# The last block of a down projection, with its norm, scaling and stores, done for 128 tokens and then for the other 128

## The chip, the cores and the metric

The kernel runs on one core of one Trainium2 chip. The metric is the device time of one execution, in microseconds (us); given are the median and the ends of three runs. The engines are PE (TensorE's products; PEld is its loading of weights), DVE (VectorE), ACT (ScalarE), POOL (GpSimd) and SP (SyncE, whose queue issues most DMAs).

## The reference, cut to what matters

One layer of a diffusion backbone with D_MODEL = 2048 channels and 256 tokens. The end of it is a SwiGLU FFN with 5632 hidden units, a gated residual and a last RMSNorm over the channels of each token:

```python
def rmsnorm(x, w):
    xf = x.astype(jnp.float32)
    y = xf * lax.rsqrt(jnp.mean(xf * xf, axis=-1, keepdims=True) + NORM_EPS)
    return (y * w.astype(jnp.float32)).astype(x.dtype)

def swiglu(h, w_gate_up, w_down):
    gate, up = jnp.split(h @ w_gate_up, 2, axis=-1)
    return (jax.nn.silu(gate) * up) @ w_down
...
        x = x + gt2 * swiglu(modulate(rmsnorm(x, norm2_w[layer]), sh2, sc2),
                             ffn_w_gate_up[layer], ffn_w_down[layer])
...
    return rmsnorm(x, final_norm_w)
```

The change touches the product with `w_down`, the residual and the last `rmsnorm`, no other part.

## The kernel before

Activations lie with channels on the 128 partitions and tokens along the free dimension (T = 256). A product takes 128 x 128 weights as its stationary operand and moves 256 token columns past them. All big products are done in a type that PE multiplies in one pass, fp32r, with two parts for each operand: a rounded high part and the rest. Three products stand for one exact one (`gemm`, L436 to L438): high weights by high activations, high weights by low activations, low weights by high activations. In the trace an fp32r product is one record, and each has its own load of weights (LDWEIGHTS, on PEld).

The weights come from HBM as fp32. `load_w` loads pieces of at most 8 chunks of 128 x 128 into a raw buffer (`wraw`, three of them, SP queue, L421); ACT casts the piece to the high part (`whi`, L426), and DVE subtracts for the low part (`wlo`, L427). There are two buffers of `whi` and two of `wlo`, so ACT's cast of a piece waits until PE is done with the piece two before it, and a load waits until DVE is done with the raw piece three before it.

The down projection (L1981 to L1991) is a loop over 16 blocks j of 128 output channels. Each sums 44 chunks of the hidden units (`Z`: `za` holds the first 32, `zb` the other 12), 132 products into one PSUM bank `mm`; its pieces have 7, 7, 8, 7, 7 and 8 chunks. Then DVE adds the gated result to the residual x1 (L1987), ACT squares it (L464), DVE adds the square to `ssum` (L1990, not for the last block), and ACT multiplies the block by its norm weights (L1991). After the loop `rms_scale` sums the squares over the partitions with two fp32 products by a matrix of ones into the bank `pa` (L455; the first takes `ssum`, the second the last block's square) and takes r by Ln and Exp on ACT (L457, L458). Five scalings on DVE multiply x1 by r (L1994), 4, 4, 4, 2 and 2 blocks of channels each, and each is followed by its store (L1995, SP queue).

`x1`, `ssum`, the squares and r are slices of one buffer, which the trace calls `arena`; `CR` holds the ones, `mod` the gates, `PR` the norm weights. `Hf` (`hfh`, `hfl`) is the input of the FFN, 16 x 256 columns for each of its two parts, last read by the products of the up projection.

The order of the instructions of each engine is set by a scheduler at build time, from its own estimate of a timeline; at run time each engine goes through its own in that order.

Of the kernel before, what the change touches and what calls it, by code (L numbers as in the profile page):

```python
# [328 lines left out]
def emit(ctx: ExitStack, tc, A, out, dbg=None):  # L329
# [29 lines left out]
    def p_(name, i=None, rows=P):  # L359
        lo, hi = _P[name]  # L360
        if i is None:
            return PR[:rows, lo:hi]
        return PR[:rows, lo + i:lo + i + 1]
# [14 lines left out]
    def pst(pool, tag, shape=None):  # L378
        return pool.tile([P, 512], F32, tag=tag, name=tag)
# [27 lines left out]
    def load_w(src, M, nk, kchunk=8, ks=0, into=None):  # L407

        res = []
        pieces = -(-(nk - ks) // kchunk)  # L410
        ends = [ks + (nk - ks) * (i + 1) // pieces for i in range(pieces)]
        for k0, k1 in zip([ks] + ends, ends):
            n = k1 - k0
            if into is None:
                raw = wpool[0].tile([P, 8, P], F32, tag="wraw", name="wraw", bufs=wbufs[0])
                hi = wpool[0].tile([P, 8, P], F32R, tag="whi", name="whi", bufs=wbufs[1])
                lo = wpool[0].tile([P, 8, P], F32R, tag="wlo", name="wlo", bufs=wbufs[2])
            else:
                raw = into[2].tile([P, 8, P], F32, tag="wr", name="wr")
                hi, lo = (t[:, k0:k1] for t in into[:2])  # L420
            ld = Q.dma_start(raw[:, :n, :M], src[:, k0:k0 + n, :])  # L421
            if into is not None:
                tc.keep_in_program_order(ld)
            for i in range(0, n, wstep[0]):
                c = slice(i, min(i + wstep[0], n))
                S.copy(hi[:, c, :M], raw[:, c, :M])  # L426
                V.tensor_sub(lo[:, c, :M], raw[:, c, :M], hi[:, c, :M].bitcast(F32))  # L427
            for k in range(n):
                res.append((k0 + k, hi[:, k, :M], lo[:, k, :M]))
        return res  # L430

    def gemm(ps, wt, X, n, first=True, last=True):

        Xh, Xl = X
        for i, (k, hi, lo) in enumerate(wt):
            E.matmul(ps, hi, Xh[:, k, :n], start=first and i == 0, stop=False)  # L436
            E.matmul(ps, hi, Xl[:, k, :n], start=False, stop=False)  # L437
            E.matmul(ps, lo, Xh[:, k, :n], start=False, stop=last and i == len(wt) - 1)  # L438

    def split(hi, lo, src):  # L440
        S.copy(hi, src)
        V.tensor_sub(lo, src, hi.bitcast(F32))
# [1491 lines left out]
    with tc.tile_pool(name="fp", bufs=1, reuse_waits="tile") as fp:  # L1934
        Hf = (fp.tile([P, KT, T], F32R, name="hfh"), fp.tile([P, KT, T], F32R, name="hfl"))
        s2 = x1p.tile([P, 16], F32, name="s2")
        V.scalar_tensor_tensor(s2, mod[:, 64:80], 1.0, p_("n2"), ALU.add, ALU.mult)
        for k in range(KT):
            hb = x1p.tile([P, T], F32, tag="m", name="hb")
            V.scalar_tensor_tensor(hb, x1[:, k, :], s2[:, k:k + 1], r, ALU.mult, ALU.mult)  # L1940
            S.activation(Hf[0][:, k, :], hb, AF.Identity, bias=mod[:, 48 + k:49 + k])
            V.scalar_tensor_tensor(Hf[1][:, k, :], hb, mod[:, 48 + k:49 + k], Hf[0][:, k, :].bitcast(F32),
                                   ALU.add, ALU.subtract)
        p4 = [pst(pmm, "mm") for _ in range(2)]
        for k in range(KT):
            for a in range(4):

                gemm(p4[a // 2][:, T * (a % 2):T * (a % 2) + T], w4[a][k:k + 1], Hf, T,
                     k == 0 and a % 2 == 0, k == KT - 1 and a % 2 == 1)
        Z = (zap.tile([P, 2, 32, T], F32R, tag="za", name="za"), fp.tile([P, 2, NH - 32, T], F32R, name="zb"))  # L1950
        cb = x1p.tile([P, 4, 512], F32, name="cb")
        Q.dma_start(cb, A["cvec"].partition_broadcast(P).rearrange("p (a d) -> p a d", a=4))
        graw = x1p.tile([P, 16, 4], F32, name="graw")
        for j in range(NH):
            if j < 2:
                ps = p4[j]
            else:
                ps = pst(pmm, "mm")
                gemm(ps[:, 0:T], load_w(A["wgu"][2 * j], P, KT), Hf, T)
                gemm(ps[:, T:512], load_w(A["wgu"][2 * j + 1], P, KT), Hf, T)  # L1960
            g = fp.tile([P, T], F32, tag="g", name="g", bufs=2)
            S.activation(g, ps[:, 0:T], AF.Silu)
            V.tensor_mul(g, ps[:, T:512], g)
            split(Z[j // 32][:, 0, j % 32], Z[j // 32][:, 1, j % 32], g)
            if j == 1:
                tc.keep_in_program_order(S.activation(cb, cb, AF.Silu))
            if 2 <= j < 34:

                for a in range(2):
                    c = (j - 2) // 2  # L1970
                    i = 2 * (j % 2) + a
                    w = fp.tile([P, 512], F32, tag="aw", name="aw", bufs=3)
                    S.dma_start(w, A["ada_gt2"][c, :, 512 * i:512 * i + 512])
                    tc.keep_in_program_order(V.scalar_tensor_tensor(w, w, 1.0, cb[:, i, :], ALU.mult, ALU.mult,
                                                                    accum_out=graw[:, c, i:i + 1]))

        V.tensor_add(graw[:, :, :2], graw[:, :, :2], graw[:, :, 2:])
        V.tensor_add(graw[:, :, 0], graw[:, :, 0], graw[:, :, 1])
        V.tensor_add(mod[:, 80:96], graw[:, :, 0], p_("bada")[:, 80:96])
        tc.keep_in_program_order(S.preload_act_table_set(LNEXP))  # L1980
        for j in range(KT):  # L1981
            ps = pst(pmm, "mm")
            wt = load_w(A["wdn"][j], P, NH)
            for i, z in enumerate(Z):
                gemm(ps[:, 0:T], [(k - 32 * i, hi, lo) for k, hi, lo in wt if k // 32 == i],
                     (z[:, 0], z[:, 1]), T, i == 0, i == 1)
            V.scalar_tensor_tensor(x1[:, j, :], ps[:, 0:T], mod[:, 80 + j:81 + j], x1[:, j, :], ALU.mult, ALU.add)  # L1987
            sq = square_sum(x1p, x1[:, j, :], ssum, j == 0)
            if 0 < j < KT - 1:
                V.tensor_add(ssum, ssum, sq)  # L1990
            S.activation(x1[:, j, :], x1[:, j, :], AF.Identity, scale=p_("nf", j))  # L1991
        r = rms_scale(x1p, [ssum, sq], T, "rs")
        for k0, k1 in ((0, 4), (4, 8), (8, 12), (12, 14), (14, 16)):
            V.tensor_mul(x1[:, k0:k1], x1[:, k0:k1], r.unsqueeze(1).to_broadcast([P, k1 - k0, T]))  # L1994
            Q.dma_start(out[:, k0:k1, :], x1[:, k0:k1, :])  # L1995


def layouts(x, c, ctx, c_ctx, w_ada, b_ada, norm1_w, w_in, rw_mu, rw_w0, rw_w2, rw_a0, rw_a2,
# [93 lines left out]
```

## Time and profile before

| what | value |
|---|---|
| median of 3 runs | 2189.06 us (2189.04 to 2196.04) |
| the profiled execution, first to last instruction (span) | 2188.6 us; the page gives no other time for it, so the runs' median stands 0.4 us above its span |
| PE busy | 2108.6 us, 96% of the span, 24536 products |
| DVE, ACT busy | 1552.5 us, 1118.2 us |
| mean granted clock of PE | 0.986 of full speed |
| from the last product of the down projection to the end | 2176.97 to 2188.63, 11.66 us |

Busy time is the time in which an engine has an instruction running; the ends of matmuls are modelled, so their pace is read from their starts. The stretch in the last line is the only one of some length at the end in which PE has almost nothing to do.

### The profile page before, as it was taken

How to read it: one execution, taken by the hardware profiler on the slowest of the kernel's cores; microseconds unless marked ns; L12 is line 12 of the kernel's file. 1: busy time of each engine (PE TensorE's matmuls, PEld its weight loads, DVE VectorE, ACT ScalarE, POOL GpSimd, SP SyncE). 2: the span in 40 equal slices, each digit the busy share in tenths (PEclk: the TensorE clock that was granted, in tenths of full speed). 3: DMA queues.
4: the chain of work that ended last, by engine and by line, in shares of the span. 5: the costliest groups of instructions: out<-in, count | busy, mean ns of one | idle time of the engine just before them, and what ended most of it. 6: DMA issues, size and time to landing. Idle time of an engine off the chain costs nothing.

```text
span 2188.6 us, 59116 instructions
## 1 busy us (share of the span) xinstructions
PE 2108.6 (96%) x24536; PEld 1977.7 (90%) x24536; DVE 1552.5 (71%) x3308; ACT 1118.2 (51%) x2209; POOL 19.2 (1%) x55
## 2 busy tenths in 40 slices
PE   7999999999999999999999998999999999999997
PEld 5897698889888888998989987999999999999997
DVE  4466589889889976899998776865666665555554
ACT  3246654565455556565565754644444444444443
POOL 0000000000000000000000000000000000000000
PEclk9999999999999999999999999999999999999999
DMA  9966756645555554665653754856777776666665
GB/s 377 415 175 196 228 154 179 178 144 156 154 167 143 166 164 135 188 194 171 176 152 112 216 153 157 297 177 201 238 248 235 242 241 217 194 191 194 195 194 163
DMA packets 276286, 431.14 MB, mean 197 GB/s; under 512 B 119857, under 2 KB 136625, under 8 KB 271665
## 3 DMA queue, kind: packets, MB, share of 16 engines
q1 hardware_dynamic: 262192, 402.19, 59.5%
q10 hardware_dynamic: 13824, 25.17, 3.6%
q8 instruction: 192, 3.15, 0.6%
q14 instruction: 78, 0.63, 0.1%
HBM read 401.50 MB, written 25.77 MB: 195 GB/s over the span
## 4 chain that ended last, share of the span: by engine, by line
PE 80%; DVE 7%; DMA 7%; ACT 3%; issue 2%; SPq 0%; DVEq 0%; ACTq 0%
PE mm L164 26%; PE mm L438 12%; PE mm L436 12%; PE mm L437 12%; PE s L164 6%; PE pa L164 5%; PE pi L164 3%; DVE arena L164 2%; DMA wraw<-w 2%; DVE wlo L164 2%; DMA wraw<-ada_rest 1%; PE mm L529 1%; PE s L579 1%; ACT arena L164 1%; PE mm L579 1%
## 5 line engine op out<-in xcount | busy, mean ns | idle before, releaser
L427 DVE TENSOR_TENSOR wlo<-wraw,whi 128x1024 fp32r<-128x1024 f32 (+1 forms) x264 | 314.9, 1193 | 291.0 <-ACT whi L426 291.0
L426 ACT CAST whi<-wraw 128x1024 fp32r<-128x1024 f32 (+1 forms) x264 | 270.6, 1025 | 386.1 <-PE mm L437 359.5
L164 PE MATMUL mm<-hxh,wlo 128*128 128x256 f32 x1376 | 399.9, 291 | 9.5 <-DVE wlo L164 7.7
L164 PE MATMUL mm<-hxh,whi 128*128 128x256 f32 x1376 | 397.0, 288 | 2.3 <-ACT whi L164 1.3
L164 PE MATMUL mm<-hxl,whi 128*128 128x256 f32 x1376 | 395.4, 287 | 0.0
L438 PE MATMUL mm<-hfh,wlo 128*128 128x256 f32 x1344 | 371.8, 277 | 0.2 <-DVE wlo L427 0.2
L436 PE MATMUL mm<-hfh,whi 128*128 128x256 f32 x1344 | 371.2, 276 | 0.0
L437 PE MATMUL mm<-hfl,whi 128*128 128x256 f32 x1344 | 371.2, 276 | 0.0
L164 ACT CAST whi<-wraw 128x512 fp32r<-128x512 f32 (+1 forms) x398 | 242.8, 616 | 214.9 <-PE mm L164 93.2
L164 DVE TENSOR_TENSOR wlo<-wraw,whi 128x512 fp32r<-128x512 f32 (+1 forms) x398 | 270.3, 682 | 86.2 <-ACT whi L164 79.8
L164 PEld LDWEIGHTS mm<-hxh,wlo 128*128 128x128 f32 x1376 | 260.7, 189 | 19.6 <-DVE wlo L164 11.3
L164 PEld LDWEIGHTS mm<-hxh,whi 128*128 128x128 f32 x1376 | 260.6, 189 | 10.3 <-issue 4.3
L164 PEld LDWEIGHTS mm<-hxl,whi 128*128 128x128 f32 x1376 | 260.8, 190 | 6.3 <-issue 3.9
L438 PEld LDWEIGHTS mm<-hfh,wlo 128*128 128x128 f32 x1344 | 252.4, 188 | 1.2 <-DVE wlo L427 0.8
L437 PEld LDWEIGHTS mm<-hfl,whi 128*128 128x128 f32 x1344 | 252.5, 188 | 0.0
L436 PEld LDWEIGHTS mm<-hfh,whi 128*128 128x128 f32 x1344 | 252.4, 188 | 0.0
L164 PE MATMUL mm<-hch,wlo 128*128 128x256 f32 x496 | 142.5, 287 | 0.0
L164 PE MATMUL mm<-hcl,whi 128*128 128x256 f32 x496 | 142.2, 287 | 0.0
L436 PE MATMUL mm<-za,whi 128*128 128x256 f32 x512 | 141.5, 276 | 0.0
L164 PE MATMUL mm<-hch,whi 128*128 128x256 f32 x496 | 141.3, 285 | 0.2 <-issue 0.2
L438 PE MATMUL mm<-za,wlo 128*128 128x256 f32 x512 | 141.3, 276 | 0.0
L437 PE MATMUL mm<-za,whi 128*128 128x256 f32 x512 | 141.3, 276 | 0.0
(407 smaller groups left out, 4534.2 us busy)
## 6 DMA issues: line engine op xcount, KB each, us to landing
wraw<-w SPq DMA_DIRECT2D x344, 256.0 KB, 3.3
wraw<-wgu SPq DMA_DIRECT2D x168, 512.0 KB, 4.7
aw<-ada_first SPq DMA_DIRECT2D x32, 1024.0 KB, 12.2
wraw<-wdn SPq DMA_DIRECT2D x64, 448.0 KB, 3.7
wraw<-ada_rest SPq DMA_DIRECT2D x96, 256.0 KB, 3.2
aw<-ada_rest SPq DMA_DIRECT2D x48, 512.0 KB, 4.4
wraw<-wout SPq DMA_DIRECT2D x64, 256.0 KB, 5.7
aw<-ada_gt ACTq DMA_DIRECT2D x64, 256.0 KB, 5.0
```

The lines of the kernel that those rows point to most:

```text
L164: return Op(self, cost, lambda: getattr(self.engine, name)(out, *a, **k), mode, base)
L426: S.copy(hi[:, c, :M], raw[:, c, :M])
L427: V.tensor_sub(lo[:, c, :M], raw[:, c, :M], hi[:, c, :M].bitcast(F32))
L436: E.matmul(ps, hi, Xh[:, k, :n], start=first and i == 0, stop=False)
L437: E.matmul(ps, hi, Xl[:, k, :n], start=False, stop=False)
L438: E.matmul(ps, lo, Xh[:, k, :n], start=False, stop=last and i == len(wt) - 1)
L529: E.matmul(ps[32 * g:32 * g + 32, 0:P], ckr[:, k].rearrange("p a b -> p (a b)"), aws[e, c][:, i, g], start=k == 0, stop=k == KT - 1)
L579: E.matmul(ps[:m, T * a:T * a + T], w_, X[:, 2 * e + k, :], start=e == k == i == 0, stop=e == NE - 1 and k == 1 and i == len(todo) - 1)
```

## The change

The loop runs over 15 blocks as before. Block 15 is written out. Its first 16 chunks are loaded by `load_w` in two pieces of 8; the other 28 in four pieces of 7, each split into a part of `Hf`, which is free by then, so that all 44 chunks of weights stay in place. Then everything is done twice, for 128 tokens each (`c` = 0 and 128): 132 products of 128 columns into a bank of their own, the add, the square, the two products by ones, Ln and Exp, four scalings (2, 4, 5 and 5 blocks) and four stores.

```diff
-    def gemm(ps, wt, X, n, first=True, last=True):
+    def gemm(ps, wt, X, n, first=True, last=True, c=0):
...
-            E.matmul(ps, hi, Xh[:, k, :n], start=first and i == 0, stop=False)
-            E.matmul(ps, hi, Xl[:, k, :n], start=False, stop=False)
-            E.matmul(ps, lo, Xh[:, k, :n], start=False, stop=last and i == len(wt) - 1)
+            E.matmul(ps, hi, Xh[:, k, c:c + n], start=first and i == 0, stop=False)
+            E.matmul(ps, hi, Xl[:, k, c:c + n], start=False, stop=False)
+            E.matmul(ps, lo, Xh[:, k, c:c + n], start=False, stop=last and i == len(wt) - 1)
...
-        for j in range(KT):
+        def down(ps, wt, n=T, c=0):
+            for i, z in enumerate(Z):
+                gemm(ps[:, c:c + n], [(k - 32 * i, hi, lo) for k, hi, lo in wt if k // 32 == i],
+                     (z[:, 0], z[:, 1]), n, i == 0, i == 1, c)
+
+        for j in range(KT - 1):
...
-        r = rms_scale(x1p, [ssum, sq], T, "rs")
-        for k0, k1 in ((0, 4), (4, 8), (8, 12), (12, 14), (14, 16)):
-            V.tensor_mul(x1[:, k0:k1], x1[:, k0:k1], r.unsqueeze(1).to_broadcast([P, k1 - k0, T]))
-            Q.dma_start(out[:, k0:k1, :], x1[:, k0:k1, :])
+
+        j = KT - 1
+        wt = load_w(A["wdn"][j, :, 0:16], P, 16)
+        wide = [t.rearrange("p k (a m) -> p (k a) m", m=P) for t in Hf]
+        for k0 in range(16, NH, 7):
+            raw = wp.tile([P, 8, P], F32, tag="wraw", name="wraw", bufs=3)[:, :7]
+            Q.dma_start(raw, A["wdn"][j, :, k0:k0 + 7])
+            hi, lo = (t[:, k0 - 16:k0 - 9] for t in wide)
+            split(hi, lo, raw)
+            wt += [(k0 + k, hi[:, k], lo[:, k]) for k in range(7)]
+        r = x1p.tile([P, T], F32, tag="rs", name="rs")
+        sq = x1p.tile([P, T], F32, tag="sq", name="sq", bufs=3)
+        for c in (0, P):
+            o = slice(c, c + P)
+            ps = pst(pmm, "mm")
+            down(ps, wt, P, c)
+            V.scalar_tensor_tensor(x1[:, j, o], ps[:, o], mod[:, 80 + j:81 + j], x1[:, j, o], ALU.mult, ALU.add)
+            S.activation(sq[:, o], x1[:, j, o], AF.Square)
+            pn = pst(pa, "pa")
+            for i, part in enumerate((ssum, sq)):
+                E.matmul(pn[:, 0:P], ones, part[:, o], start=i == 0, stop=i == 1)
+            S.activation(x1[:, j, o], x1[:, j, o], AF.Identity, scale=p_("nf", j))
+            S.activation(r[:, o], pn[:, 0:P], AF.Ln, bias=eps, scale=1.0 / D)
+            S.activation(r[:, o], r[:, o], AF.Exp, scale=-0.5)
+            for k0, k1 in ((0, 2), (2, 6), (6, 11), (11, 16)):
+                V.tensor_mul(x1[:, k0:k1, o], x1[:, k0:k1, o], r[:, o].unsqueeze(1).to_broadcast([P, k1 - k0, P]))
+                Q.dma_start(out[:, k0:k1, o], x1[:, k0:k1, o])
```

The scheduler places the new instructions. On PE, where block 15 goes from its first piece of weights to its second, the kernel before has these rows (the bank `mm_28354` is block 15's; `whi` and `wlo` carry the numbers of the pieces):

```order
L438 MATMUL mm_28354<-za_20258,wlo_28357 128x256
L436 MATMUL mm_28354<-za_20258,whi_28362 128x256 [waits Activation_49]
L437 MATMUL mm_28354<-za_20258,whi_28362 128x256
L438 MATMUL mm_28354<-za_20258,wlo_28363 128x256 [waits DVE_49]
L436 MATMUL mm_28354<-za_20258,whi_28362 128x256
```

In the changed kernel the same place reads as follows; `mm_28382` is the bank of the first 128 tokens, `mm_28531` that of the second, and `28355` and `28356` are the first piece's two parts, `28361` and `28362` the second's:

```order
L438 MATMUL mm_28531<-za_20258,wlo_28356 128x128
L436 MATMUL mm_28382<-za_20258,whi_28361 128x128 [waits Activation_49]
L437 MATMUL mm_28382<-za_20258,whi_28361 128x128
L436 MATMUL mm_28531<-za_20258,whi_28355 128x128
L437 MATMUL mm_28531<-za_20258,whi_28355 128x128
...
L436 MATMUL mm_28531<-za_20258,whi_28355 128x128
L438 MATMUL mm_28382<-za_20258,wlo_28362 128x128 [waits DVE_49]
L436 MATMUL mm_28382<-za_20258,whi_28361 128x128
```

So the halves are not strictly one after the other: 12 products of the second half, on the first piece's weights, stand ahead of the second piece's high part, and 10 more ahead of its low part. After the first half's last product 110 of the second half's 132 are left, and the first half's two products by ones stand 25 products apart among them.

On ACT, around the end of block 14 (whose last pieces are `28207` and `28213`), the kernel before has

```order
L426 CAST whi_28213<-wraw_28212 128x1024 [waits DMAHW7_49,DVE_49,PE_49]
L426 CAST whi_28356<-wraw_28355 128x896 [waits DMAHW0_49,DVE_49,PE_49]
L426 CAST whi_28362<-wraw_28361 128x896 [waits DMAHW1_49,DVE_49,PE_49]
L464 ACTIVATE arena_1603<-arena_1603 128x256 [waits DVE_49]
L1991 ACTIVATE arena_1603<-arena_1603,PR_82 128x256 [waits Activation_49]
L426 CAST whi_28368<-wraw_28367 128x1024 [waits DMAHW2_49,PE_49]
```

and the changed one

```order
L426 CAST whi_28213<-wraw_28212 128x1024 [waits DMAHW7_49,DVE_49,PE_49]
L426 CAST whi_28355<-wraw_28354 128x1024 [waits DMAHW0_49,DVE_49,PE_49]
L441 CAST hfh_20013<-wraw_28366 128x896 [waits DMAHW2_49]
L426 CAST whi_28361<-wraw_28360 128x1024 [waits DMAHW1_49,DVE_49,PE_49]
L464 ACTIVATE arena_1603<-arena_1603 128x256 [waits DVE_49]
L1993 ACTIVATE arena_1603<-arena_1603,PR_82 128x256 [waits Activation_49]
L441 CAST hfh_20013<-wraw_28370 128x896 [waits DMAHW3_49]
```

The cast of the third piece, which goes to `hfh` and waits for its DMA alone, has moved ahead of the cast of the second; the subtractions on DVE stand in the same order, with block 14's add (L1989) ahead of the third piece's.

On SP, at the end of the program, the difference is

```order
-L421 DMA wraw<-wdn 128x1024
-L421 DMA wraw<-wdn 128x896 x2
-L421 DMA wraw<-wdn 128x1024
-L421 DMA wraw<-wdn 128x896 x2
-L421 DMA wraw<-wdn 128x1024
-L1995 DMA out<-arena 128x1024 x3
-L1995 DMA out<-arena 128x512 x2
-L2087 UNCONDITIONAL_BRANCH
+L421 DMA wraw<-wdn 128x1024 x3
+L2000 DMA wraw<-wdn 128x896 x4
+L2020 DMA out<-arena 128x2x128
+L2020 DMA out<-arena 128x4x128
```

followed by six more stores at L2020. The loads keep their number; the five stores have become eight, with 512 bytes in a row where there were 2048 or more.

## Rows read from the trace of the kernel before

**Rows 1.** The page: busy us of each engine, its share and instructions.

```profile
PE 2108.6 (96%) x24536; PEld 1977.7 (90%) x24536; DVE 1552.5 (71%) x3308; ACT 1118.2 (51%) x2209; POOL 19.2 (1%) x55
```

**Rows 2.** Busy us by stretch, each with its instructions; then PEclk, DMA share, GB/s.

```profile
2161.40:2176.97 15.57, 15.55 (x135) 15.30 (x134) 6.55 (x7) 5.75 (x7) 0.00 (x0) 1.00 0.32 98
2176.97:2188.63 11.66, 0.70 (x2) 0.30 (x2) 5.18 (x6) 1.81 (x4) 0.00 (x0) 0.66 0.46 180
```

**Rows 3.** The chain that ended last: start, us, what; the kernel's end.

```profile
2166.27 0.43 PE pa L455 x2
...
2176.99 0.49 DVE arena L1987
2177.51 0.42 ACT arena L464
2177.98 0.71 PE pa L455 x2
2178.71 0.48 ACT arena L457
2179.22 0.42 ACT arena L458
2179.67 1.23 DVE arena L1994
```

**Rows 4.** Timeline of PE, first and last of 27 products (start, us, what).

```profile
2173.73 0.28 PE L436 MATMUL mm<-zb,whi 128*128 128x256 f32 x1
...
2176.67 0.28 PE L438 MATMUL mm<-zb,wlo 128*128 128x256 f32 x1
```

**Rows 5.** Timeline of PEld: ten 128-column loads for products of 32 or 64 columns.

```profile
799.58 0.30 PEld L164 LDWEIGHTS pa<-gtok,C 128*128 128x128 f32 x2
...
800.25 0.53 PEld L164 LDWEIGHTS pa<-gtok,CR 128*128 128x128 f32 x4
800.70 0.19 PEld L164 LDWEIGHTS mm<-hxh,wlo 128*128 128x128 f32 x1
```

**Rows 6.** Timeline of PE: eight fp32 products of 128 columns in a row.

```profile
877.36 1.05 PE L164 MATMUL pa<-arena 128*128 128x128 f32 x8
```

**Rows 7.** PEld by line and shape: busy us, mean ns of one.

```profile
L436 PEld LDWEIGHTS mm<-za,whi 128*128 128x128 f32 x512 | 96.1, 188 | 0.0
...
L164 PEld LDWEIGHTS pa<-gtok,CR 128*128 128x128 f32 x6 | 0.8, 192 | 0.0
```

**Rows 8.** Timeline of ACT, DVE and SP where block 15 begins.

```profile
2158.71 0.94 ACT L426 CAST whi<-wraw 128x896 fp32r<-128x896 f32 x1 [1.33 <-PE mm L437]
...
2157.41 1.23 DVE L427 TENSOR_TENSOR wlo<-wraw,whi 128x1024 fp32r<-128x1024 f32 x1 [1.40 <-ACT whi L426]
2161.54 0.48 DVE L1987 SCALAR_TENSOR_TENSOR arena<-mm,mod,arena 128x256 f32<-128x256 f32 x1 [0.77 <-PE mm L438]
2162.41 1.09 DVE L427 TENSOR_TENSOR wlo<-wraw,whi 128x896 fp32r<-128x896 f32 x1 [0.38 <-ACT whi L426]
...
2158.66 0.33 SPq L421 DMA_DIRECT2D wraw<-wdn  x1
```

**Rows 9.** Loads at L421 from 2140 us on: time from issue to landing.

```profile
DMA to landing us min/median/max: 3.3/3.6/3.9
```

**Rows 10.** DVE and ACT by line and shape: busy us, mean ns of one.

```profile
L164 DVE SCALAR_TENSOR_TENSOR Rg<-s,negc,gvt 128x128 f32<-128x128 f32 x48 | 16.1, 343 | 7.2 <-PE s L164 7.0
L1990 DVE TENSOR_TENSOR arena<-arena 128x256 f32<-128x256 f32 x14 | 5.9, 419 | 0.0
L1994 DVE TENSOR_TENSOR arena<-arena 128x1024 f32<-128x1024 f32 x3 | 3.5, 1220 | 2.2 <-ACT arena L458 2.2
...
L164 ACT ACTIVATE arena<-arena 128x128 f32<-128x128 f32 x3 | 0.9, 309 | 0.0
```

**Rows 11.** The stores: issues at L1995, and time to landing.

```profile
L1995 SPq DMA_DIRECT2D out<-arena x5: 333/344/707, 2180.9 to 2184.4; - x5
DMA to landing us min/median/max: 2.7/3.0/3.1
```

More of the change, by code (lines that the diff above doesn't have):

```diff
@@ L1980, in emit @@
         tc.keep_in_program_order(S.preload_act_table_set(LNEXP))
-        for j in range(KT):
+        def down(ps, wt, n=T, c=0):
[3 more added lines that the diff above has]
+        for j in range(KT - 1):
             ps = pst(pmm, "mm")
[L1983 to L1986, printed above, removed]
+            down(ps, load_w(A["wdn"][j], P, NH))
@@ L1987, in emit @@
             V.scalar_tensor_tensor(x1[:, j, :], ps[:, 0:T], mod[:, 80 + j:81 + j], x1[:, j, :], ALU.mult, ALU.add)
             sq = square_sum(x1p, x1[:, j, :], ssum, j == 0)
-            if 0 < j < KT - 1:
+            if j:
                 V.tensor_add(ssum, ssum, sq)
             S.activation(x1[:, j, :], x1[:, j, :], AF.Identity, scale=p_("nf", j))
-        r = rms_scale(x1p, [ssum, sq], T, "rs")
-        for k0, k1 in ((0, 4), (4, 8), (8, 12), (12, 14), (14, 16)):
-            V.tensor_mul(x1[:, k0:k1], x1[:, k0:k1], r.unsqueeze(1).to_broadcast([P, k1 - k0, T]))
-            Q.dma_start(out[:, k0:k1, :], x1[:, k0:k1, :])
+        j = KT - 1
```

## The prediction

> **What bounds the kernel now.** I read the page first: PE is busy for 2108.6 us, 96% of the span [rows 1], so whatever adds time to PE adds it to the kernel, except where PE has nothing left to do. That is only at the end. The second view is the busy time by stretch, cut at the end of the last product [rows 2]: block 15 of the down projection fills PE (15.55 of 15.57 us, clock 1.00), and in the 11.66 us after it PE works for 0.70 us. The third is the chain that ended last [rows 3], which takes these 11.66 us apart: add of the block 0.49, square 0.42, two passes over ones 0.71, Ln 0.48, Exp 0.42, which with the gaps is 2.70 us from 2176.97 to the first scaling at 2179.67; then five scalings (3 x 1.220 and two of half the size, about 0.69 each by the slope between 256 and 1024 columns, [rows 10]: 5.0 by sum, 4.7 as the last store's issue at 2184.4 shows, [rows 11]). The last store lands 3.0 us later [rows 11], and 1.2 us are left to the end at 2188.63. So tail = 2.70 + 4.70 + 0.05 + 3.00 + 1.21 = 11.66. The profiled execution has this span; the median of the runs is 2189.06, so 0.4 us lie around it, and I take them as unchanged.
>
> **What the change removes.** The last 128 tokens alone stand in the tail now. From the last product to the first scaling, with 128 columns: the add 0.34 instead of 0.49 (nearest row, a 128-column one out of PSUM [rows 10]); square, Ln and Exp about 0.31 each (the 128-column ACT row [rows 10]) instead of 0.42, 0.48 and 0.42; the two passes over ones 0.39 (0.11 from one start to the next and 0.28 for the last, from eight such in 1.05 us [rows 6]) instead of 0.71. With the same gaps that is 2.70 - 0.15 - 0.11 - 0.17 - 0.11 - 0.32 = 1.9 us (rounded up, since one of the gaps is a wait on ACT). The scalings go over 256, 512, 640 and 640 elements: 0.42 + 0.69 + 0.82 + 0.82 = 2.75 us by the slope from 419 ns to 1220 ns [rows 10]. The last store is of 320 KB in pieces of 512 bytes, a form that the stores of before don't have; its bounds are 2.7 us, the quickest store [rows 11], and 3.9 us, the slowest load of 448 to 512 KB [rows 9]; I take 3.0, as now. Tail after: 1.9 + 2.75 + 0.05 + 3.0 + 1.2 = 8.9 us, **2.8 us less** (1.9 to 3.1). The first 128 tokens' norm, scaling and stores run while PE multiplies for the second, so they cost nothing on ACT, DVE and SP; without that cover they would cost another tail.
>
> **What it adds on PE.** 132 products of 256 columns become 264 of 128, each with its own load of 128 weight columns. Now a product starts every 0.113 us (26 intervals from 2173.73 to 2176.67 [rows 4]). If a product's price went with its columns, two of 128 would cost the same as one of 256. The trace has no product of this type (fp32r) with 128 columns, so the price is bounded: 0.057 below (half of 0.113), and above by two fp32 records, 0.22 (each written fp32 product shows as two records, [rows 3], of 0.111 each [rows 6]). What decides is how fast weights can be loaded. [Rows 5] show it for fp32: ten loads of 128 columns, from 799.58 to 800.70, one every 0.112 us, although the products that they feed move only 32 or 64 columns. There the stream is too short to matter; the load is the price. The load of fp32r weights shows as long as that one (188 against 192 ns [rows 7]), and both are 4 bytes an element. So I take **0.112 us** for a product of 128 columns, nearly as much as one of 256 costs now; the eight fp32 products, whose streams are as long as their loads, say 0.111 [rows 6]. Then PE needs 264 x 0.112 = 29.6 us. The passes over ones for the first half are two program rows, four records of 0.111, 0.4 us; the pair for the second half is in the tail above, its first one hidden behind the add. Together 30.0 us from block 15's first product to its last; now it is 15.5, from 2161.45 (block 14's add, which waits for PE, starts at 2161.54 [rows 8]) to 2176.97: **14.5 us more**, with 0.111 to 0.113 as bounds 14.2 to 14.8.
>
> The Trainium skill (TensorE: Matmul & The Clock Gate, section Weight-path perf modes — Fast Weight Load (FWL) and DoubleRow) says that a fast weight load is on where 128 weights are loaded and the input isn't FP32, and that FP32 has no gain from it. It does not say which of the two fp32r is; the like durations in rows 7 speak for no gain. The Trainium skill (TensorE: Matmul & The Clock Gate, section Back-to-back issue gap) also gives about 81 ns for each pair of load and product with 128 columns, which no row of this trace shows; an estimate by it is 264 x 0.081 = 21.4 us, some 8 us less than the sum above, and so about 2192.6.
>
> **What it moves.** The first two loads of block 15, A and B, are of 8 chunks; the other 28 chunks, C to F, go to the space of the FFN's input, which nothing reads any more. ACT now casts C before B. C's load goes into the raw buffer of block 14's last piece, which DVE leaves at 2157.41 + 1.23 = 2158.64, so it is issued at 2158.66 [rows 8] and lands 3.6 us later [rows 9], at 2162.3; today ACT would cast at about 2161.4 there, when block 14 ends. So B's cast, the square and the scaling of block 14 wait behind C: cast C to 2163.2, cast B (1.05, of 8 chunks) to 2164.3. On DVE the difference of C (1.09 [rows 8]) stands before that of B (1.23), so B's second part is ready at 2165.6. That would hold PE up for about 1.3 us if it did the halves one after the other: A lasts only to 2161.45 + 24 x 0.112 = 2164.1. But PE's order puts 22 products of the second half, on A's weights, ahead of B's second part: it comes up as the 49th, at 2161.45 + 48 x 0.112 = 2166.8, so the delay is covered, with 1.2 us to spare. D to F come later still: E, whose raw buffer is B's, is loaded from 2165.6, lands at 2169.2, is split at 2171.3 and is wanted as the 113th product, at 2174.0; F is split at 2172.4 and wanted at 2176.3. I put this at zero, and at most 1 us. The first half's pass over ones on the square comes 25 products after its last product, 2.8 us, against some 0.9 us for add and square: covered too.
>
> **Sum.** 14.5 - 2.8 = 11.7 us: 2188.6 + 11.7 = 2200.3 for the span, and 2189.06 + 11.7 = **2200.8 us** for the median. Bounds of this case: 14.2 - 3.1 = 11.1 and 14.8 + 1.0 - 1.9 = 13.9, so 2200.2 to 2203.
>
> **Rivals.**
> 1. *The narrow product costs half (0.057).* Then the loads of fp32r weights take less than 0.057 us, against rows 7. PE has 15 us of work, and the weights bound the first half: F is split at 2172.4, its 21 products end at 2173.7; 110 products of the second half are left, 6.2 us, and 0.4 for the passes: 2180.4. With the tail of 8.9, 2189.3, so +0.6: **2189.7**. It decides against me if the interval is under 0.10. Even here the kernel isn't faster by 11 us: the whole tail is 11.66 us, and no more than 3.1 of it goes.
> 2. *Load and stream share the time, halfway (0.084).* 264 x 0.084 + 0.4 = 22.6 us, with about 0.4 of waiting for E: 7.5 more than now, less 2.8: **2193.8**.
> 3. *fp32r falls back to the fp32 price when narrow (0.22).* 264 x 0.222 = 58.6: +43.5 - 2.8, **2229.8**. Nothing in the trace speaks for it but that no narrow fp32r product is there.
> 4. *C's load is late.* If C lands 1.5 us later or more, B passes the cover of 1.2 us, and PE waits; each further us is a us on the path: **2202 to 2203**, in the range of my case.
>
> **How the numbers follow.** My case has 0.74 (with rival 4), rival 1 0.08, rival 2 0.10, rival 3 0.08. The predicted time is my case's. 0.5% of this kernel is 10.9 us, about what a measurement of it can tell from no change, and my case lies at 11.7, just beyond; with its bounds I give it 3 to 1 to end beyond. Slower by over 0.5%: 0.74 x 0.75 + 0.08 = 0.63; within 0.5%: the rest of my case and rivals 1 and 2, 0.34; faster: 0.03, for what I haven't seen. The range takes in my case and rivals 1 and 2, 2190 to 2204, and leaves out rival 3 and a few in a hundred of rival 1.
>
> **What would show it.** In the profile of the changed kernel, the loads and products of 128 columns in the last 40 us start every 0.111 to 0.113 us, with no wait on PE at B; the last product ends about 30 us after block 15's first; the chain from there to the end takes 8.9 us, with scalings of 0.42 to 0.82 us; PE's busy share stays 9 tenths where the first half's stores run. Intervals near 0.06 or 0.08 would make the prediction wrong on the fast side, near 0.22 on the slow side; a last store far over 3 us would add to the tail.

## The result, and the profile after

| kernel | runs | median us (lowest to highest) | ratio to before, 95% interval |
|---|---|---|---|
| before | 6 | 2189.73 (2189.04 to 2196.04) | 1 |
| changed | 6 | 2203.73 (2200.69 to 2208.85) | 1.0058 (1.0042 to 1.0073) |

The changed kernel is slower by 0.58%, 12.7 us by the ratio, between 9.2 and 16.0 by its interval. Predicted were 2200.8 us, a plus of 11.7, and slower by over 0.5% as the likeliest sign.

Its page answers to [rows 1] (busy us of each engine, share, instructions):

```profile
span 2206.3 us, 59396 instructions
PE 2120.7 (96%) x24672; PEld 1988.0 (90%) x24672; DVE 1552.3 (70%) x3312; ACT 1119.1 (51%) x2213; POOL 19.2 (1%) x55
```

PE has 136 instructions more: 132 products, and four records of the second pair of fp32 passes over ones. This execution took 2208.07 us, 1.8 us more than its span; so much lies around the span in every run of it.

The busy time by stretch, cut at the end of the last product, answers to [rows 2] (PE, PEld, DVE, ACT, POOL, then the granted clock, DMA share and GB/s):

```profile
2167.57:2197.61 30.04, 30.04 (x272) 30.04 (x270) 9.14 (x12) 6.82 (x11) 0.00 (x0) 1.00 0.29 83
2197.61:2206.30 8.69, 0.76 (x4) 0.37 (x3) 2.85 (x5) 1.39 (x4) 0.00 (x0) 0.75 0.43 121
```

Block 15 fills PE for 30.04 us without a pause at the full clock; its tail is 8.69 us. Before, the same two stretches are 15.63 us and 11.66 [rows 2]; the block's first product there starts at

```profile
2161.34 0.28 PE L436 MATMUL mm<-za,whi 128*128 128x256 f32 x1
```

So the block costs 14.4 us more, the tail gives back 3.0, and block and tail together take 38.73 us instead of 27.29: **+11.4**. The rest of this profiled run's difference stands before the block: it starts at 2167.57 instead of 2161.34, behind work that the change leaves alone. In nine other profiles below, of kernels alike up to there but for what e5_early and e8_pinned load or split earlier, block 15 starts anywhere from 2159.7 to 2174.3. I therefore compare each kernel from that start on. (The seven profiles with the changed kernel's loads start it at 2164.5 to 2174.3, the four with those of before at 2159.7 to 2165.2. Whether the change itself shifts the start by a us or so, single profiles can't show.)

The timeline of PE, DVE and ACT answers to [rows 4] and [rows 8]: the block's first products, those around the 49th, the last one; then DVE, ACT and the load of C (on SP's queue) at the block's start.

```profile
2167.57 0.22 PE L436 MATMUL mm<-za,whi 128*128 128x128 f32 x1
...
2172.76 0.28 PE L436 MATMUL mm<-za,whi 128*128 128x128 f32 x1
2172.88 0.27 PE L438 MATMUL mm<-za,wlo 128*128 128x128 f32 x1
...
2197.33 0.28 PE L438 MATMUL mm<-zb,hfl 128*128 128x128 f32 x1
...
2169.92 1.09 DVE L442 TENSOR_TENSOR hfl<-wraw,hfh 128x896 fp32r<-128x896 f32 x1 [1.67 <-ACT hfh L441]
2170.93 1.22 DVE L427 TENSOR_TENSOR wlo<-wraw,whi 128x1024 fp32r<-128x1024 f32 x1
...
2168.95 0.94 ACT L441 CAST hfh<-wraw 128x896 fp32r<-128x896 f32 x1 [2.97 <-DMA wraw<-wdn]
2169.79 1.04 ACT L426 CAST whi<-wraw 128x1024 fp32r<-128x1024 f32 x1
...
2164.89 7.61 SPq L2000 DMA_DIRECT2D wraw<-wdn  x4
```

A narrow product starts every 0.111 to 0.112 us. ACT casts C before B, after 2.97 us of waiting for C's load; B's low part is ready at 2172.15, and PE takes it up at 2172.88, 0.7 us later.

The chain that ended last answers to [rows 3] (start, us, what; L2019 is the scaling, DVEq its queue):

```profile
2197.64 0.36 DVE arena L2010
2198.03 0.32 ACT arena L2011
2198.39 0.50 PE pa L2014 x2
2198.91 0.38 ACT arena L2016
2199.31 0.32 ACT arena L2017
2199.65 0.43 DVE arena L2019
2200.08 0.60 DVEq L2112
2200.68 1.47 DVE arena L2019 x2
```

From the last product's end at 2197.61 to the first scaling it is 2.04 us, the scalings take 2.50, and from there to the end it is 4.15. The stores answer to [rows 11] (issues, KB each, median us to landing; tail and first half together):

```profile
out<-arena SPq DMA_DIRECT2D x4, 320.0 KB, 3.0
```

And a scaling of 640 elements, by line and shape, takes the 0.82 us that the slope in [rows 10] gave:

```profile
L2019 DVE TENSOR_TENSOR arena<-arena 128x640 f32<-128x640 f32 x4 | 3.1, 819 | 0.0
```

### The profile page after: what moved, and what is told of

Same layout as the page of the kernel before. It is cut to its first block, busy times and chain, and to the rows that moved or that the text cites. A ratio compares the mean times of both kernels' runs of the same rounds, so it can differ in the third digit from the quotient of the medians.

```text
span 2206.3 us, 59396 instructions
## 1 busy us (share of the span) xinstructions
PE 2120.7 (96%) x24672; PEld 1988.0 (90%) x24672; DVE 1552.3 (70%) x3312; ACT 1119.1 (51%) x2213; POOL 19.2 (1%) x55
## 4 chain that ended last, share of the span: by engine, by line
PE 78%; DMA 9%; DVE 7%; ACT 3%; issue 2%; SPq 1%; ACTq 0%; DVEq 0%
PE mm L164 27%; PE mm L438 12%; PE mm L436 12%; PE mm L437 11%; PE s L164 6%; PE pa L164 5%; DMA wraw<-w 3%; PE pi L164 3%; DVE arena L164 2%; DVE wlo L164 2%; DMA wraw<-wgu 2%; PE mm L529 1%; PE s L579 1%; PE mm L579 1%; DMA wraw<-w_low 1%
## 5 line engine op out<-in xcount | busy, mean ns | idle before, releaser
L437 PE MATMUL mm<-za,whi 128*128 128x256 f32 (+1 forms) x512 | 141.2, 276 | 0.0
L436 PE MATMUL mm<-za,whi 128*128 128x256 f32 (+1 forms) x512 | 141.1, 276 | 0.0
L438 PE MATMUL mm<-za,wlo 128*128 128x256 f32 (+1 forms) x512 | 141.1, 276 | 0.0
```

The lines of the kernel that those rows point to most:

```text
L436: E.matmul(ps, hi, Xh[:, k, c:c + n], start=first and i == 0, stop=False)
L437: E.matmul(ps, hi, Xl[:, k, c:c + n], start=False, stop=False)
L438: E.matmul(ps, lo, Xh[:, k, c:c + n], start=False, stop=last and i == len(wt) - 1)
```

## The experiments

The theory going in: a load of 128 columns of fp32r weights, with its product, costs 0.112 us whatever number of columns the product moves, so splitting the block's columns doubles PE's work there, and the split of the tail gives back too little. The rivals: the price goes with the columns, or the time is lost in the new order (C ahead of B) or in the stores. The last column of the summary is what carries the comparison; all times are us. The runs were made on several chips, so the first column is no comparison by itself; a ratio in the text is to runs of the kernel before on the same chip.

| kernel | time (runs) | first product of block 15 to start of its last | from there to the end | together |
|---|---|---|---|---|
| before, profiled | 2189.73 (6) | 15.33 | 11.96 | 27.29 |
| changed | 2203.73 (6) | 29.76 | 8.96 | 38.72 |
| e2_narrow | 2202.77 (1) | 29.32 | 11.95 | 41.27 |
| e3_quarter | 2288.77 (1) | 107.88 | 9.39 | 117.27 |
| e4_order | 2231.68 (1) | 54.73 | 9.39 | 64.11 |
| e5_early | 2228.94 (1) | 53.27 | 9.40 | 62.67 |
| e8_pinned | 2203.29 (10) | 29.76 | 8.96 | 38.72 |
| e1_wide | 2193.09 (12) | 16.63 | 12.94 | 29.57 |
| e6_lead | 2194.79 (1) | 17.90 | 11.72 | 29.62 |
| e7_stores | 2189.53 (12) | 15.33 | 11.78 | 27.11 |

**The narrow products alone (e2_narrow).** The kernel before, with only block 15's products halved, in one bank; loads, norm, scaling and stores as before.

```diff
+                        for a, (w, X) in enumerate(((hi, z[:, 0]), (hi, z[:, 1]), (lo, z[:, 0]))):
+                            for c in (0, P):
+                                E.matmul(ps[:, c:c + P], w, X[:, k - 32 * i, c:c + P],
+                                         start=k == a == c == 0, stop=k == NH - 1 and a == 2 and c == P)
```

> The kernel before, with one edit: each of block 15's 132 products is done as two of 128 columns in the same bank, and loading, norm, scaling and stores stay as they were. If a narrow product costs what the load of its weights costs, 264 x 0.112 = 29.6 us stand in place of 15.0, and from block 15's first product to the end it takes 27.2 + 14.6 = 41.8 us. If the added time of the change comes from the loads' new order, from the parts kept in the FFN's input or from the stores, it stays at 27 to 28 us.

Busy time by stretch:

```profile
2159.70:2189.29 29.59, 29.59 (x267) 29.59 (x266) 6.54 (x7) 5.74 (x7) 0.00 (x0) 1.00 0.18 53
2189.29:2200.97 11.68, 1.18 (x4) 0.37 (x3) 5.18 (x6) 1.82 (x4) 0.00 (x0) 0.63 0.46 180
```

PE has 14.0 us more from first start to last start, and the tail is that of before: the whole loss is there without any of the moved loads, and the rival of the columns falls. The changed kernel's 29.76 is this 29.32 and 0.44 for the first half's passes over ones.

**The price of a load by width (e9_prices).** The changed kernel with 84 dead products of each width after the last ones, on weights and activations that lie in place (`wb` and `zb` are bf16 copies of two such tiles); nothing reads their results. It took 2324.34 us in one run, the dead products included.

```diff
+            for n in (256, 224, 192, 160, 128, 96, 64, 32):
+                pt = pst(psq, "s")
+                for k in range(28):
+                    for a in range(3):
+                        E.matmul(pt[:, :n], wide[a == 2][:, k], Z[0][:, a == 1, k, :n], start=k == a == 0, stop=k == 27 and a == 2)
+            for n in (256, 128, 64, 32):
...
+                        E.matmul(pt[:, :n], wb, zb[:, :n], start=k == a == 0, stop=k == 27 and a == 2)
```

> The changed kernel, with products behind its last ones whose results nothing reads, 84 for each width: fp32r with 256, 224, 192, 160, 128, 96, 64 and 32 columns, then with both operands in bf16 (one chunk of weights) 256, 128, 64 and 32. If the load is the price, fp32r takes 0.112 us from 32 up to about 250 columns and 0.113 at 256; with half pace when narrow it falls from 0.2 at 224 columns to 0.03 at 32; with a price by columns from 0.113 to 0.014. For bf16, whose weights have half the bytes, I have no row; under 0.07 at 128 columns would put the price down to the four bytes of the type, 0.11 to the 128 weight columns alone. PE's clock may fall where it isn't full.

Timeline of PE: the first and the last record of the fp32r products with 224, 128 and 64 columns, 84 of each:

```profile
2214.72 0.38 PE L2030 MATMUL s<-za,hfh 128*128 128x224 f32 x2
2223.98 0.27 PE L2030 MATMUL s<-za,hfl 128*128 128x224 f32 x1
...
2242.82 0.37 PE L2030 MATMUL s<-za,hfh 128*128 128x128 f32 x2
2252.07 0.28 PE L2030 MATMUL s<-za,hfl 128*128 128x128 f32 x1
...
2265.62 0.60 PE L2030 MATMUL s<-za,hfh 128*128 128x64 f32 x2
2283.31 0.40 PE L2030 MATMUL s<-za,hfl 128*128 128x64 f32 x1
```

Over 83 intervals that is 9.26 us, 0.1116 each, with 224 columns, and 9.25 us, 0.1114 each, with 128: the price doesn't move with the columns. With 64 it is 17.69 us, 0.213 each; but that is at half the clock, as the stretches show (columns as above). At the full clock the next run has 0.112 for 64 columns:

```profile
2205.00:2257.10 52.10, 52.10 (x464) 52.10 (x462) 2.50 (x4) 1.14 (x4) 0.00 (x0) 1.00 0.08 21
2257.10:2304.90 47.80, 47.80 (x227) 46.80 (x227) 0.00 (x0) 0.00 (x0) 0.00 (x0) 0.50 0.00 1
```

The clock fell at 2257.1 amid the products of 96 columns (which run from 2252.19), with PE busy all the time, and came back at 2304.9, among those of 256 bf16 columns. The bf16 products, by line and shape:

```profile
L2035 PE MATMUL s<-wz 128*128 128x128 bf16 x84 | 4.9, 219 | 0.0
...
L2035 PE MATMUL s<-wz 128*128 128x32 bf16 x84 | 2.3, 176 | 0.0
```

4.9 us of busy time for 84 is at most 0.058 each, half the price of fp32r with as many columns, and 2.3 us with 32 columns is at most 0.027. Each of these products has its own record of a load, if always of the same weights; so a bf16 load takes no longer than 0.027 us, and there the price falls with the columns. What the fp32r runs show is a fixed price for a load with its product: no run here has fp32r products that share a load, so the load isn't told apart from some other fixed cost of such a pair. The Trainium skill (TensorE: Matmul & The Clock Gate, section Weight-path perf modes — Fast Weight Load (FWL) and DoubleRow) has FP32 without the fast load; the trace agrees, and puts fp32r on FP32's side, 0.111 against 0.058. The 81 ns that the Trainium skill (TensorE: Matmul & The Clock Gate, section Back-to-back issue gap) gives for a pair with 128 columns is met by neither; the measurement decides. Left open: the fp32r products of 256 columns, on weights in `hfh` and `hfl`, started every 0.120 us in the median here, against 0.113 in the blocks [rows 4]. In e1_wide below both stand in one block: 0.120 on `hfh` and `hfl`, 0.113 to 0.114 on `whi` and `wlo`. So it goes with the tile that holds the weights; why is not shown.

**Products of 64 columns (e3_quarter).** The changed kernel, each product of 128 columns as two of 64.

```diff
+                            for q in (c, c + 64):
+                                E.matmul(ps[:, q:q + 64], w, X[:, k - 32 * i, q:q + 64],
+                                         start=k == a == 0 and q == c, stop=k == NH - 1 and a == 2 and q > c)
```

> The changed kernel, with each product of 128 columns done as two of 64. If the price is that of the load, 128 weight columns whatever is moved past them, 528 x 0.112 = 59.1 us stand in place of 29.6, and from block 15's first product to the end it takes 38.7 + 29.6 = 68.3 us. The rival theory, that products narrower than 256 columns move at half the pace (twice the time for each column, the load hidden), gives 0.056 for 64 columns, 29.6 us in all, and 38.7 us as in the changed kernel.

Busy time by stretch:

```profile
2169.71:2175.48 5.77, 5.77 (x55) 5.77 (x53) 4.05 (x5) 3.54 (x5) 0.00 (x0) 1.00 0.54 153
2175.48:2277.59 102.11, 102.11 (x481) 102.11 (x481) 5.12 (x8) 3.26 (x6) 0.00 (x0) 0.50 0.05 16
```

In the first stretch the products of 64 columns start every 0.112 us, which is the theory's price (0.056 would be the rival's). Then, without a pause on PE, the clock falls to 0.50 (1.2 GHz) and stays there, and a product takes 0.213 (102.11 us for about 480). Both expectations miss the total, 117.3: neither had the clock in it.

**The order written out (e4_order).** The changed kernel; PE does the first half's 132 products, then 24 of the second, the passes over ones, and the other 108. So the 22 products that cover B are no longer ahead of B's low part.

```diff
+        with tc.manual_schedule(engines={mybir.EngineType.PE}):
+            banks = [pst(pmm, "mm") for _ in range(2)]
+            part(banks[0], 0, 0, NH)
+            part(banks[1], P, 0, 8)
+            rest(0, banks[0])
+            part(banks[1], P, 8, NH)
+            rest(P, banks[1])
```

> The changed kernel, with PE's order written out: all products of the first half, 24 of the second, the first half's two products by ones, the rest of the second. If the second half's 22 products do cover the late second piece of weights, PE now waits there for about 1.3 us (0.5 to 2.5), and from block 15's first product to the end it takes 40.0 us. If that piece wasn't late at all, 38.7 us as in the changed kernel.

Timeline of PE around B's low part:

```profile
2168.52 0.28 PE L437 MATMUL mm<-za,whi 128*128 128x128 f32 x1
2169.63 0.33 PE L438 MATMUL mm<-za,wlo 128*128 128x128 f32 x1 [0.83 <-DVE wlo L427]
...
2170.12 0.28 PE L436 MATMUL mm<-za,whi 128*128 128x128 f32 x1
2170.24 0.34 PE L437 MATMUL mm<-za,whi 128*128 128x128 f32 x1
2170.38 0.42 PE L438 MATMUL mm<-za,wlo 128*128 128x128 f32 x1
2170.59 0.41 PE L436 MATMUL mm<-za,whi 128*128 128x128 f32 x1
```

Busy time by stretch, before and after the intervals change:

```profile
2165.79:2170.30 4.51, 3.68 (x34) 3.54 (x33) 3.37 (x5) 3.54 (x5) 0.00 (x0) 1.00 0.51 132
2170.30:2200.00 29.70, 29.70 (x141) 29.70 (x141) 4.54 (x7) 3.26 (x6) 0.00 (x0) 0.50 0.08 28
```

The wait is there as foreseen: 1.1 us between two starts instead of 0.11. What follows it was not: at 2170.3 the intervals go from 0.11 to 0.21 and stay so to the end, at a clock of 0.50. The wait itself costs 1.0 us; block and tail take 25.4 us more than in the changed kernel.

**An own raw buffer for C (e5_early).** As e4_order, with a buffer of its own for C's raw weights, so that its load needn't wait.

```diff
+            if k0 == 16:
+                raw = fp.tile([P, 7, P], F32, name="raw2")
+            else:
+                raw = wp.tile([P, 8, P], F32, tag="wraw", name="wraw", bufs=3)[:, :7]
```

> The changed kernel with PE's order written out as in e4_order, and a raw buffer of its own for the third piece, so that its load is there early and the second piece's cast is not behind it. If it was the wait of 1.1 us at the second piece that let PE's clock fall for the rest of the block, the wait is 0.2 us or less here, the clock stays at 2.4 GHz and the last stretch takes 38.7 us. If the strict order itself (no other reason for idling) brings the clock down, it takes 67 us again.

Timeline of PE and ACT:

```profile
2168.76 0.33 PE L438 MATMUL mm<-za,wlo 128*128 128x128 f32 x1 [0.88 <-DVE wlo L427]
...
2165.51 0.94 ACT L441 CAST hfh<-wraw 128x896 fp32r<-128x896 f32 x1 [2.60 <-DMA wraw<-wdn]
2166.36 1.04 ACT L426 CAST whi<-wraw 128x1024 fp32r<-128x1024 f32 x1
```

C's split went far ahead, but the scheduler then put D, which still uses a shared buffer, in C's old place in front of B. PE waits for B as in e4_order, and the clock falls at 2171.5. The edit didn't remove the wait, so it doesn't tell order and wait apart; it repeats e4_order with another load in the way.

**The same order without the wait (e8_pinned).** PE's order of e4_order, with the casts and subtractions of A, B and C written in that order, B's ahead of C's.

```diff
+        def last(*pieces):
+            for k0, k1 in pieces:
...
+                Q.dma_start(raw, A["wdn"][KT - 1, :, k0:k1])
+                tc.keep_in_program_order(S.copy(hi, raw))
+                tc.keep_in_program_order(V.tensor_sub(lo, raw, hi.bitcast(F32)))
...
+            if j == KT - 2:
+                last((0, 8), (8, 16), (16, 23))
```

> The changed kernel with PE's order written out, as in e4_order, and on ACT and DVE the second piece's cast and subtraction pinned ahead of the third's, so that its low part is ready 2.4 us after block 15 begins and wanted at 2.9 us. If the wait for that piece is what brought PE's clock down in e4_order and e5_early, there is no gap over 0.3 us, the clock stays at 2.4 GHz to the end of the block, and from block 15's first product to the end it takes 38.7 us (38 to 40); in the runs' times 11 to 14 us over the kernel before. If one half after the other by itself lets the clock fall, 60 us or more again.

Busy time by stretch, with the place of B in the first:

```profile
2166.71:2171.20 4.49, 4.49 (x43) 4.49 (x42) 3.14 (x4) 3.42 (x5) 0.00 (x0) 1.00 0.60 149
2171.20:2196.70 25.50, 25.50 (x230) 25.50 (x230) 6.04 (x8) 3.59 (x7) 0.00 (x0) 1.00 0.23 72
```

2203.29 us over 10 runs, ratio 1.0045 (1.0029 to 1.0061), and 38.72 us for block and tail, those of the changed kernel. The order costs nothing in itself; with the order of PE the same in both, e4_order (one run) lost its time by the wait for B and what followed it. It also shows that the change gains nothing from interleaving the halves, if B is ready.

**Wide products, the rest as changed (e1_wide).** 132 products of 256 columns, then add, norm, scaling and stores in halves; the six loads of the change.

```diff
+        ps = pst(pmm, "mm")
+        down(ps, wt)
         for c in (0, P):
             o = slice(c, c + P)
-            ps = pst(pmm, "mm")
-            down(ps, wt, P, c)
```

> The changed kernel, with block 15's products kept 256 columns wide in one bank (132 of them); loading, the norm in halves, the eight scalings and stores are the change's. If the narrow products are the cost, PE needs 15.0 us, and about 1.4 us of waiting for the second piece's low part, which nothing covers here; the tail of both halves, whose stores of 512-byte pieces ran at 290 GB/s in the changed kernel, takes about 12 us: 28 to 30 us from block 15's first product to the end, about 1 to 2 us over the kernel before. If PE's clock falls in that wait as it did with the order written out, wide products should bring it back, at a cost of 2 to 4 us. The rival, that staging and halves cost by themselves, gives 36 us or more.

Timeline of PE at B:

```profile
2169.62 0.28 PE L437 MATMUL mm<-za,whi 128*128 128x256 f32 x1
2170.70 0.38 PE L438 MATMUL mm<-za,wlo 128*128 128x256 f32 x1 [0.81 <-DVE wlo L427]
```

Busy time in the stretch behind it:

```profile
2170.70:2183.58 12.88, 12.88 (x108) 12.88 (x109) 3.56 (x4) 2.21 (x3) 0.00 (x0) 1.00 0.21 70
```

Timeline of DVE (the eight scalings), and the view of the DMAs from 2180 to 2196.2 in 40 slices:

```profile
2185.89 4.91 DVE L2019 TENSOR_TENSOR arena<-arena 128x256 f32<-128x256 f32 x8 [1.66 <-ACT arena L2017]
...
GB/s 0 0 0 0 0 0 0 0 0 0 0 0 0 0 0 0 0 10 279 157 260 304 278 293 283 279 293 286 280 284 291 277 293 285 288 290 168 0 0 0
```

2193.09 us over 12 runs, ratio 1.0010 (0.9996 to 1.0024); +2.3 us in block and tail. 1.3 of it lies in the block: 1.2 for the wait and the intervals beside it and 0.6 for the 84 products on `hfh` and `hfl`, less some 0.4 for the passes over ones on `ssum`, which stand inside the block before and behind it here. 1.0 lies behind the last product's start, and it isn't the two norms: the first scaling comes 2.6 us after that start, sooner than before (3.0), and the scalings take 4.9 us instead of 4.7. But from the end of the scalings to the end of the span it is 5.4 us instead of 4.3: the stores in pieces of 512 bytes are still moving. Nearly the same wait as in e4_order, 1.08 us between starts, but among wide products the clock stays at 1.00. Without the narrow products nearly all of the loss of the change is gone, and so is its gain.

**Only the last 8 chunks in halves (e6_lead).** The kernel before with 108 wide products and 24 narrow ones for each half.

```diff
+        down(ps, wt[:36])
+        V.scalar_tensor_tensor(x1[:, j, :], ps[:, 0:T], mod[:, 80 + j:81 + j], x1[:, j, :], ALU.mult, ALU.add)
...
+            down(ps, wt[36:], P, c)
```

> The kernel before (its own loads), with only the last piece of block 15, 8 chunks, done in halves of 128 tokens (24 products as 48), and the norm, scaling and stores in halves. PE pays 24 x 0.110 = 2.7 us more and 0.4 for the products by ones; the first half has a lead of 2.7 us, and the tail falls from 11.7 to about 9.5: 27 to 29 us from block 15's first product to the end, no better than the 27.2 of the kernel before. The theory that a narrow product costs its columns gives 25 us.

Timeline of PE (the first half's pass over ones on its square) and DVE (the eight scalings):

```profile
2181.36 0.44 PE L2008 MATMUL pa<-arena,CR 128*128 128x128 f32 x2
2182.63 4.91 DVE L2013 TENSOR_TENSOR arena<-arena 128x256 f32<-128x256 f32 x8 [0.72 <-ACT arena L2011]
```

2194.79 us in one run. PE takes 2.6 us more (24 loads more, 2.7) and what follows its last product's start is 11.72, only 0.2 shorter. What was expected there, a tail of 9.5, was wrong, for two reasons that the trace shows. PE's order puts the first half's pass over ones behind the second half's last product (2181.26), 1.55 us after its square was done (2179.81): so the first scaling starts 1.4 us after that product's start, where it was 3.0 before, and none of the scalings is covered. And from the end of the eight scalings to the end of the span it is 5.4 us, as in e1_wide, instead of 4.3.

**The stores cut otherwise (e7_stores).** The kernel before, whose scalings and stores take 1, 2, 3, 4, 3 and 3 blocks.

```diff
-        for k0, k1 in ((0, 4), (4, 8), (8, 12), (12, 14), (14, 16)):
+        for k0, k1 in ((0, 1), (1, 3), (3, 6), (6, 10), (10, 13), (13, 16)):
```

> The kernel before, with one edit: the scalings and stores take 1, 2, 3, 4, 3 and 3 blocks of channels in place of 4, 4, 4, 2 and 2. The stores are bound by their 2.1 MB at 400 GB/s once the first has begun, and the first begins after a scaling of 0.42 us in place of 1.22: 0.4 to 0.8 us less in the tail, 26.4 to 26.9 us from block 15's first product to the end. In the runs' times that is under 0.05% and can't be told from no change.

Ratio 0.9994 (0.9981 to 1.0006) over 12 runs: no difference that these runs can tell, as foreseen. In the stretch it is 0.2 us less, where 0.4 to 0.8 were expected.

## Why the prediction was right

The mechanism came as predicted, and the time lies in the range, but with some luck: 2203.73 us is 0.3 us below the range's end and 0.7 above the 2200.2 to 2203 that I had worked out as the bounds of my own case, and the six runs alone spread over 8 us. The sign, slower by over 0.5%, holds for the ratio of 0.58%; its interval begins at 0.42%. Step by step:

- **The price of a narrow product, the step that decides.** 0.112 was read from loads for fp32 [rows 5] and carried over to fp32r by their like durations [rows 7]. The changed kernel shows 0.1115 in the mean (29.76 us less 0.44 for the passes, over 263 intervals), e9_prices 0.1114. That the load alone makes the price is argued from this, not shown. The block: 30.04 us against 30.0 predicted; the plus is 14.4 against 14.5. e2_narrow shows that it comes from the products alone. Rivals 1, 2 and 3 (0.057, 0.084, 0.22) fall with it.
- **The tail.** 8.69 us against 8.9; the gain is 3.0, not 2.8. The way to the first scaling took 2.04 instead of 1.9, the scalings 2.50 instead of 2.75: I summed their durations, though before they already overlapped (5.0 by sum, 4.7 by the last issue), and should have taken the overlap over. The last stores land after 3.0 us as assumed.
- **The sum.** +11.4 us in block and tail against +11.7. The ratio's +12.7 includes both within its interval; what lies between stands in front of block 15, where single profiles of like work scatter by more.
- **The time around the span** was mis-sized. I took 0.4 us, from the median beside a span of another execution. It is 1.8 us, so the profiled execution of before took about 2190.4 us, and the span's 2200.3 would go with 2202.1. The forecast itself was added to the median of the runs and doesn't use this term. Of the 3.0 us by which it is low, 0.7 is that median, which became 2189.73 with three runs more; the other 2.3 is what the medians differ by, 14.0, beyond my 11.7, and as block and tail measure 11.4, it doesn't come from there. Where it comes from is not shown; it is small beside the spread of the runs.
- **The moved loads.** C's cast started 1.4 us after the block's start, where I had 0.85: its load was issued at 2164.89, and the cast waited for it until 2168.95, 4.06 us and not 3.6. B's low part was therefore ready 4.6 us after the start and not 4.15, and the cover left 0.7 us to spare instead of 1.2. E's and F's low parts came at 9.9 and 11.0 us after the start, as worked out (9.85 and 10.95), and no product waits for them.
- **Rival 4 failed in its price.** I wrote that each further us of a late B "is a us on the path". Two profiles show otherwise: in e4_order and e5_early a wait of some 1.1 us for B is followed by half the clock, and block and tail take 24 to 25 us more than in the changed kernel. Had C landed some 2 us later, the time could have been near 2230, outside my range (argued from these two profiles, each the only run of its kernel). All six runs of the changed kernel lie at 2200.7 to 2208.9, so it didn't happen; that it stands only 0.7 us away was not in my chances. Why the clock stays low is not shown beyond these profiles.

Does a smaller split pay? Worked out, not run: the first half's norm and scalings, 2.0 + 2.5 us, need cover from the second half's products, 4.5 / 0.112 = 40 of them, and those 40 are 40 loads more, 4.5 us, for a gain of 3.0. The stores in small pieces would need cover too, by e1_wide and e6_lead 1.2 us more at the end without it. e6_lead is the case with less cover, though PE's order kept it from using what it had; the changed kernel is the one with more. No kernel here was measurably faster than before.

## What to carry to other kernels

Before splitting the moving columns of a product, read the start interval of products whose streams are short: it is what a load and its product cost whatever moves, and if the whole product costs no more than that, each split in two doubles it. Weigh what a shorter tail can give at most against that, here 3.0 us for 14.4. And look at the waits among such narrow products: their own length is not what they cost if the clock falls behind them.

## What the runs showed of the hardware that I had not expected

- The granted clock fell from 1.00 (2.4 GHz) to 0.50 (1.2 GHz) behind a wait of 1.1 us among products of 128 columns (e4_order, e5_early), and PE, busy without a pause after it (29.70 of 29.70 us), did not get it back in the rest of the block. Among products of 256 columns a wait of nearly the same length (e1_wide) left it at 1.00.
- It fell with no wait at all among fp32r products of 64 columns (e3_quarter) and of 96 columns (e9_prices), and returned among bf16 products of 256 columns. Those of 128 columns, without a wait, kept 1.00 for the whole block (changed kernel, e8_pinned, e2_narrow).
- At half the clock the price of a load with its product is 1.9 times that at the full clock, 0.213 against 0.112 us (e3_quarter, e4_order).
- Stores in pieces of 512 bytes move more slowly than those of before. In the view of the DMAs in 40 slices, the changed kernel from 2185 to 2207 us:

```profile
GB/s 30 0 0 0 0 0 0 0 0 92 182 270 304 279 290 291 199 0 0 0 0 0 0 0 0 0 0 0 0 230 212 282 272 300 288 287 36 0 0 0
```

The kernel before from 2176 to 2189 us:

```profile
GB/s 0 0 0 0 0 0 0 0 0 0 0 0 0 0 0 0 0 151 403 403 378 429 403 416 391 403 416 391 429 334 391 378 366 359 13 0 0 0 0 0
```

Without the first two slices and the last of each burst, 270 to 304 GB/s stand against 334 to 429. The stores of 320 KB land after 3.0 us in the median all the same; where all eight stores come in a row (e1_wide, e6_lead), the end is 1.2 us later for it. Size and number of the pieces changed together (4224 packets instead of 720), so neither is shown to be the cause by itself.
